# Encoder block in split fp32: who orders the instructions of the vector, scalar and GpSimd engines, which kind of PSUM bank each product takes, and when a block's first half is summed

## The chip, the cores and the metric

The kernel runs on one core of a Trainium2 chip. The metric is the device time of one execution in microseconds (us); lower is better. In the profile PE is TensorE, DVE is VectorE, ACT is ScalarE, POOL is GpSimd, and SP is SyncE, whose queue issues nearly all DMA transfers.

## The reference

One layer of a hybrid bidirectional encoder block: S = 256 tokens, D = 2048, DFF = 5632, all in float32. Cut to what matters:

```python
h = rms_norm(x, g_mix)
proj = h @ w_in                       # q, k, v of three mixers, and three gates of width D
oa, ob, oc = ...                      # dilated windows (6 heads), GQA with rope (6), cross attention to mem (4)
merged = sigmoid(gate_a) * (oa @ w_br_a) + sigmoid(gate_b) * (ob @ w_br_b) + sigmoid(gate_c) * (oc @ w_br_c)
x = x + merged @ w_o
hf = rms_norm(x, g_ffn) @ w_ffn_in    # 2048 x 11264
x = x + (silu(hf[..., :DFF]) * hf[..., DFF:]) @ w_ffn_out
```

Cross attention reads keys and values from `rms_norm(mem, g_mem) @ w_mem_kv`.

## The kernel before

**Arithmetic.** Every fp32 operand is split into a rounded high part and a rest (`split`): ACT copies to `hi` (in the trace `whi`, `x1T`, `hT` and so on), then DVE subtracts and writes `lo` (`wlo`, ...). A product is three matmuls into one PSUM bank: hi by hi, hi by lo, lo by hi. All weights stream through: `load` brings 512 KB (128 x 1024) into one of six buffers `raw` on SP's queue, `halves` splits it into `whi` and `wlo` (four buffers each). So each load costs ACT one copy, DVE one subtraction and PE twelve matmuls of 128x512, or fewer.

**Stages.** `beginning` (keys and values from `mem`); eight products for q, k, v, with the attention running beside them, and four products for the gates and the first branch; then `merging`, `projecting` (x plus merged by `w_o`, and x transposed into `x1T`) and `feeding`. `feeding` handles 11 blocks of `w_ffn` in groups of 4, 4 and 3; behind each group two pairs of column blocks of `w_ffn_out` are added to x.

**A pair.** `pair()` computes two column blocks of 512 at once for two token tiles, so four results: Y and V of the first column block (c = 0), Z and Q of the second (c = 1). It yields steps. A step `d` loads 128x1024 of weights for one column block and issues twelve matmuls: one d-step for Y, V, then one for Z, Q. In the blocks of `w_ffn` three of the contraction's eight parts (`SEVEN = 3`) go by seven products in place of eight: s-steps come in threes, *first* (banks X and Y), *second* (W and Z, from DVE's sums of loaded weights: `t3`, then `raw`, then `t2`), *third* (V, from one more DVE sum); steps 6 and 7 feed X from `t2` and `t3`. The order of a block is `d3 s0 d4 s1 d5 s2 6 d6 7 d7`. `SA` and `SB` hold X's and W's parts; at the end of a pair `finish_seven` adds Y, V, Z and Q to them, all four after the last step. Then `done` is called (in feeding: `hidden`, which applies silu to the first half and starts a side job: multiply the halves, then `transposed`, two groups of four 128x128 PE transposes through a bank `tp`, each emptied by ACT and DVE into `hT`).

**What sets the order.** `run()` prepares three steps ahead (`AHEAD`): a step's loads, splits and sums are issued three steps before its matmuls. `tick()` after each step moves one side job on; a job's `yield n` lets n steps pass. While `run()` runs, `nc` is the wrapper `InOrder` with `on` true: each instruction of all five engines is kept behind the one issued before it on the same engine (`keep_in_program_order`; every instruction of the trace so carries line L70 of the wrapper). The twelve products between `beginning` and `merging` are not in `run()`: there the Tile scheduler orders the engines, by a simulated timeline. Within an engine's queue instructions issue in order, so one that waits holds all behind it.

**Banks.** PSUM has eight banks, in two kinds of four that rotate: `at` and `mm`. A pair takes X, Y and W from `at` and Z, V and Q from `mm`; `tp` takes `at`. A bank is free for its next user once it is emptied.

**The beginning.** Side jobs beside the pair for `mem`: `constants` (after 10 steps: a load of `rope`, a memset of `relb` by DVE, then the load of `relb`, which waits for the memset), and `fetch(xT, 1)`, which loads and splits x transposed, for the qkv products, from step 8 on.

## Time and profile before

| | |
|---|---|
| median of 3 runs | 1478.7 us (1476.6 to 1480.47) |
| the profiled execution | 1478.82 us, span 1477.0 us, mean granted TensorE clock 0.992 |
| busy in the span | PE 1422.2 us, DVE 969.8, ACT 732.4, POOL 76.6 |
| loads of `w_ffn` | 176 of 512 KB, 3.9 us to landing (median) |
| one block of `w_ffn` | 46.4 us (the first d7 matmul at 851.43, the next block's at 897.85) |

Times in rows of the profile count from the span's start. A PE row's duration is modelled; how far matmuls are apart is read from the starts. `[1.36 <-DVE hT L70]` behind a row says that the engine was idle for 1.36 us before it, and that the last thing it waited for was DVE's instruction writing `hT`. Buffer numbers are left out of names in the profile (`hT_7051` is `hT`, `t3_6997` is `t`), and kept in the order's rows below.

### The profile page before, as it was taken

How to read it: one execution, taken by the hardware profiler on the slowest of the kernel's cores; microseconds unless marked ns; L12 is line 12 of the kernel's file. 1: busy time of each engine (PE TensorE's matmuls, PEld its weight loads, DVE VectorE, ACT ScalarE, POOL GpSimd, SP SyncE). 2: the span in 40 equal slices, each digit the busy share in tenths (PEclk: the TensorE clock that was granted, in tenths of full speed). 3: DMA queues.
4: the chain of work that ended last, by engine and by line, in shares of the span. 5: the costliest groups of instructions: out<-in, count | busy, mean ns of one | idle time of the engine just before them, and what ended most of it. 6: DMA issues, size and time to landing. Idle time of an engine off the chain costs nothing.

```text
span 1477.0 us, 17243 instructions
## 1 busy us (share of the span) xinstructions
PE 1422.2 (96%) x6323; PEld 1152.0 (78%) x6323; DVE 969.8 (66%) x1190; ACT 732.4 (50%) x981; POOL 76.6 (5%) x146
## 2 busy tenths in 40 slices
PE   8899999999999999999799999999999999999998
PEld 6678888888788888888577777887777788777776
DVE  5567777754454555646768887557888754788753
ACT  6656565544344444444455545335545533455532
POOL 0012733100000000000000000000000000000000
PEclk9999999999999999999899999999999999999999
DMA  7875455556566666655356556656555566555634
GB/s 273 318 239 186 156 164 165 157 173 197 184 188 197 196 189 190 238 174 196 100 163 208 171 173 204 194 170 201 174 187 178 188 201 196 179 173 179 210 102 169
DMA packets 79411, 277.05 MB, mean 188 GB/s; under 512 B 8992, under 2 KB 11552, under 8 KB 79072
## 3 DMA queue, kind: packets, MB, share of 16 engines
q1 hardware_dynamic: 79184, 275.94, 58.0%
q8 instruction: 49, 0.80, 0.2%
q14 instruction: 34, 0.28, 0.1%
q10 hardware_dynamic: 144, 0.02, 0.0%
HBM read 273.05 MB, written 2.88 MB: 187 GB/s over the span
## 4 chain that ended last, share of the span: by engine, by line
PE 79%; DVE 10%; ACT 6%; DMA 3%; issue 2%; POOL 1%; SPq 0%; ACTq 0%; DVEq 0%
PE mm L70 17%; PE mmY L70 15%; PE mmZ L70 14%; PE mmV L70 14%; PE mmQ L70 13%; DVE wlo L70 5%; ACT whi L70 5%; PE mmX L70 3%; DVE SA L70 1%; PE tp L70 1%; DMA raw<-in_w_mem 1%; PE mmW L70 1%; PE sc L70 1%; DMA rows<-in_x 1%; PE o L70 1%
## 5 line engine op out<-in xcount | busy, mean ns | idle before, releaser
L70 DVE TENSOR_TENSOR wlo<-raw,whi 128x1024 fp32r<-128x1024 f32 (+1 forms) x529 | 630.8, 1203 | 431.2 <-ACT whi L70 428.6
L70 ACT ACTIVATE whi<-raw 128x1024 fp32r<-128x1024 f32 (+1 forms) x529 | 537.7, 1032 | 581.1 <-PE mmQ L70 155.6
L70 PE MATMUL mm<-whi,xT 128*128 128x512 f32 x768 | 245.6, 395 | 3.4 <-ACT xT L70 3.4
L70 PEld LDWEIGHTS mm<-whi,xT 128*128 128x128 f32 x768 | 144.0, 189 | 34.2 <-ACT xT L70 3.8
L70 PE MATMUL mm<-wlo,xT 128*128 128x512 f32 x384 | 151.0, 394 | 0.8 <-DVE wlo L70 0.8
L70 PE MATMUL mmV<-whi,x1T 128*128 128x512 f32 x286 | 112.8, 395 | 0.0
L70 PE MATMUL mmY<-whi,x1T 128*128 128x512 f32 x286 | 112.8, 394 | 0.0
L70 PE MATMUL mmZ<-whi,x1T 128*128 128x512 f32 x220 | 85.7, 389 | 0.0
L70 PE MATMUL mmQ<-whi,x1T 128*128 128x512 f32 x220 | 85.6, 389 | 0.0
L70 PEld LDWEIGHTS mm<-wlo,xT 128*128 128x128 f32 x384 | 72.5, 189 | 16.0 <-DVE wlo L70 1.1
L70 PE MATMUL mmQ<-whi,hT 128*128 128x512 f32 x176 | 69.7, 396 | 2.0 <-DVE x L70 2.0
L70 PE MATMUL mmZ<-whi,hT 128*128 128x512 f32 x176 | 70.2, 399 | 1.1 <-ACT whi L70 1.1
L70 PE MATMUL mmY<-whi,hT 128*128 128x512 f32 x176 | 69.4, 394 | 0.0
L70 PE MATMUL mmV<-whi,hT 128*128 128x512 f32 x176 | 69.1, 393 | 0.0
L70 PEld LDWEIGHTS mmV<-whi,x1T 128*128 128x128 f32 x286 | 54.3, 190 | 11.3 <-ACT whi L70 0.4
L70 PE MATMUL mmY<-wlo,x1T 128*128 128x512 f32 x143 | 58.2, 407 | 4.5 <-DVE wlo L70 3.3
L70 PEld LDWEIGHTS mmY<-whi,x1T 128*128 128x128 f32 x286 | 54.0, 189 | 10.5
L70 PE MATMUL mmV<-wlo,x1T 128*128 128x512 f32 x143 | 56.7, 396 | 0.2 <-DVE wlo L70 0.2
L70 PE MATMUL mmY<-whi,xT 128*128 128x512 f32 x128 | 50.0, 391 | 0.0
L70 PE MATMUL mmZ<-whi,xT 128*128 128x512 f32 x128 | 50.0, 390 | 0.0
L70 PE MATMUL mmV<-whi,xT 128*128 128x512 f32 x128 | 49.8, 389 | 0.0
L70 PE MATMUL mmQ<-whi,xT 128*128 128x512 f32 x128 | 49.8, 389 | 0.0
(243 smaller groups left out, 2463.3 us busy)
## 6 DMA issues: line engine op xcount, KB each, us to landing
raw<-in_w_ffn SPq DMA_DIRECT2D x176, 512.0 KB, 3.9
raw<-in_w_gate SPq DMA_DIRECT2D x96, 512.0 KB, 4.0
raw<-in_w_ffn_out SPq DMA_DIRECT2D x88, 512.0 KB, 3.7
raw<-in_w_qkv SPq DMA_DIRECT2D x64, 512.0 KB, 4.4
raw<-in_w_o SPq DMA_DIRECT2D x32, 512.0 KB, 3.6
raw<-in_w_br SPq DMA_DIRECT2D x24, 512.0 KB, 3.7
raw<-in_w_mem SPq DMA_DIRECT2D x16, 512.0 KB, 6.3
rawT<-in_memT SPq DMA_DIRECT2D x8, 256.0 KB, 4.0
```

The costliest lines, as they stand in the source:

```text
L70: ins = op(*args, **kw)
```

## The change

1. `InOrder` wraps only TensorE and SyncE. DVE, ACT and POOL instructions are the scheduler's to order everywhere; PE's and SP's stay as written in `run()`.
2. X, Y and Z take `at` banks; V, Q and W take `mm` banks.
3. The second transpose group (`h = 1`) takes an `mm` bank while `nc.on`, the first an `at` bank.
4. `finish_seven` becomes `sums(c)`: Y and V are added to `SA` after the last step but one, Z and Q to `SB` after the last, each followed by `done(c, ...)`, both under `tc.high_priority()`. So silu is issued for the first half a step sooner, and the multiplication waits one step instead of two (`yield 1`), which puts both transpose groups a step forward.
5. `fetch(xT, 1)` starts after 5 steps instead of 8.

```diff
-        for name in ("tensor", "vector", "scalar", "gpsimd", "sync"):
+        for name in ("tensor", "sync"):
             setattr(self, name, self._Engine(self, getattr(tc.nc, name)))
+        for name in ("vector", "scalar", "gpsimd"):
+            setattr(self, name, getattr(tc.nc, name))
...
-            tp = bank("tp")
+            tp = bank("tp", "mm" if h and nc.on else "at")
...
-                ps[b] = bank("mm" + b, "at" if b in "XYW" else "mm")
+                ps[b] = bank("mm" + b, "at" if b in "XYZ" else "mm")
...
-        def finish_seven():
-            SA, SB = tl["A"], tl["B"]
-            nc.vector.tensor_sub(SB[:, 0], ps["Z"], SB[:, 0])
-            nc.vector.tensor_add(SA[:, 1], ps["V"], SA[:, 1])
-            nc.vector.tensor_add(SA[:, 0], ps["Y"], SA[:, 0])
-            nc.vector.tensor_add(SB[:, 1], ps["Q"], SB[:, 1])
-            return SA, SB
+        def sums(c):
+            if not seven:
+                return [ps[b] for b in ("YV", "ZQ")[c]]
+            to = tl["AB"[c]]
+            (nc.vector.tensor_sub if c else nc.vector.tensor_add)(to[:, 0], ps["YZ"[c]], to[:, 0])
+            nc.vector.tensor_add(to[:, 1], ps["VQ"[c]], to[:, 1])
+            return to
...
+            def ending(products=products, c=i + 2 - len(steps)):
+                products()
+                with tc.high_priority():
+                    done(c, sums(c))
+            yield ending
...
-        start(hold(8, fetch(xT, 1)))
+        start(hold(5, fetch(xT, 1)))
...
-                def hidden(av, bv):
+                def hidden(c, v, av=halves_of):
+                    if c == 0:
+                        av.append(v)
+                        for t in range(T):
+                            nc.scalar.activation(v[:, t], v[:, t], AF.Silu, scale=r_f[:, 0, t:t + 1])
+                        return
...
-                        yield 2
+                        yield 1
                         nc.vector.tensor_mul(av, av, bv)
```

Before, `pair` called `done(*finish_seven())` after the last step of a pair with seven products, and `done(0, ...)` and `done(1, ...)` after the last two steps of the others, as now.

**DVE at the boundary between two blocks of `w_ffn`.** Before, from the first sum for the next block's first s-step on (`SA<-SA,SB` is the product of the halves; `hT` rows empty the transposes; `[waits DMA...]` is a wait for a load):

```order
L70 TENSOR_TENSOR t3_6997<-raw_7029 128x512 [waits DMAHW1_49]
L70 TENSOR_TENSOR raw_7029<-raw_7029,raw_7027 128x512 [waits DVE_49]
L70 TENSOR_TENSOR t2_6996<-raw_7029 128x512 [waits DVE_49]
L70 TENSOR_TENSOR wlo_7058<-raw_7029,whi_7057 128x1024 [waits Activation_49]
L70 TENSOR_TENSOR SA_6906<-SA_6906,SB_6907 128x1024
L70 TENSOR_TENSOR raw_7027<-t2_6996,raw_7027 128x512 [waits DVE_49]
L70 TENSOR_TENSOR wlo_7078<-raw_7027,whi_7077 128x512 [waits Activation_49]
L70 TENSOR_TENSOR wlo_7098<-raw_7095,whi_7097 128x1024 [waits DMAHW2_49,Activation_49]
L70 TENSOR_TENSOR hT_7051<-tp_7108,hT_7051 128x512 [waits Activation_49]
L70 TENSOR_TENSOR wlo_7118<-raw_7115,whi_7117 128x1024 [waits DMAHW3_49,Activation_49]
L70 TENSOR_TENSOR wlo_7133<-raw_7128,whi_7132 128x1024 [waits DMAHW4_49,Activation_49]
L70 TENSOR_TENSOR hT_7051<-tp_7139,hT_7051 128x512 [waits Activation_49]
```

And now, from the second half's sums on:

```order
L375 TENSOR_TENSOR SB_6907<-mmZ_6724,SB_6907 128x512 [waits PE_49]
L376 TENSOR_TENSOR SB_6907<-mmQ_6728,SB_6907 128x512 [waits PE_49]
L433 TENSOR_TENSOR raw_7031<-t2_6996,raw_7031 128x512 [waits DVE_49]
L417 TENSOR_TENSOR t3_6997<-raw_7137 128x512 [waits DMAHW5_49]
L109 TENSOR_TENSOR wlo_7059<-raw_7033,whi_7058 128x1024 [waits Activation_49]
L777 TENSOR_TENSOR SA_6906<-SA_6906,SB_6907 128x1024 [waits DVE_49]
L418 TENSOR_TENSOR raw_7137<-raw_7137,raw_7135 128x512 [waits DMAHW4_49,DVE_49]
L109 TENSOR_TENSOR wlo_7078<-raw_7031,whi_7077 128x512 [waits Activation_49]
L109 TENSOR_TENSOR wlo_7105<-raw_7102,whi_7104 128x1024 [waits DMAHW2_49,Activation_49]
L419 TENSOR_TENSOR t2_6996<-raw_7137 128x512 [waits DVE_49]
L109 TENSOR_TENSOR hT_7053<-tp_7095,hT_7053 128x512 [waits Activation_49]
L109 TENSOR_TENSOR wlo_7118<-raw_7115,whi_7117 128x1024 [waits DMAHW3_49,Activation_49]
```

The sums `t3`, `raw`, `t2` of the block's first s-step have moved forward, ahead of the last step's sums; in their place stands the first of the next s-step (`t3_6997<-raw_7137`), which waits for a load, ahead of a slice and the product.

**PE at the same boundary.** Before, from the first transpose group to the second:

```order
L70 MATMUL tp_7108<-ident_77,SA_6906 128x128 x2
L70 MATMUL mmW_7121<-whi_7057,fh_5731 128x512 [waits Activation_49]
L70 MATMUL mmW_7121<-wlo_7058,fh_5731 128x512
L70 MATMUL mmW_7121<-whi_7057,fl_5732 128x512
L70 MATMUL mmZ_7081<-whi_7057,fh_5731 128x512
L70 MATMUL mmZ_7081<-wlo_7058,fh_5731 128x512
L70 MATMUL mmZ_7081<-whi_7057,fl_5732 128x512
L70 MATMUL mmV_7065<-whi_7077,x1T_5185 128x512 [waits Activation_49]
L70 MATMUL mmV_7065<-wlo_7078,x1T_5185 128x512 [waits DVE_49]
L70 MATMUL mmV_7065<-whi_7077,x1T_5185 128x512
L70 MATMUL tp_7139<-ident_77,SA_6906 128x128 [waits DVE_49]
L70 MATMUL tp_7139<-ident_77,SA_6906 128x128 x3
```

And now, first where the first group begins, then where the second stands:

```order
L70 MATMUL mmQ_7085<-whi_7011,x1T_5186 128x512
L70 MATMUL tp_7095<-ident_77,SA_6906 128x128 [waits DVE_49,Activation_49]
L70 MATMUL tp_7095<-ident_77,SA_6906 128x128 [waits Activation_49]
L70 MATMUL tp_7095<-ident_77,SA_6906 128x128 x2
L70 MATMUL mmX_7108<-whi_7035,x1T_5185 128x512
L70 MATMUL mmX_7108<-wlo_7036,x1T_5185 128x512
```

```order
L70 MATMUL mmZ_7081<-whi_7058,fh_5731 128x512
L70 MATMUL mmZ_7081<-wlo_7059,fh_5731 128x512
L70 MATMUL mmZ_7081<-whi_7058,fl_5732 128x512
L70 MATMUL tp_7128<-ident_77,SA_6906 128x128 x4
L70 MATMUL mmV_7066<-whi_7077,x1T_5185 128x512 [waits Activation_49]
L70 MATMUL mmV_7066<-wlo_7078,x1T_5185 128x512 [waits DVE_49]
```

Each group has moved a step forward, the first ahead of X and Y, the second ahead of V, and the second group's wait for DVE's eviction is gone.

**DVE in the beginning.** Before, the memset of `relb` is row 35, behind the slices of the `mem` pair:

```order
L70 TENSOR_TENSOR wlo<-raw,whi 128x1024 [waits DMAHW7_49,Activation_49]
L70 TENSOR_TENSOR wlo<-raw,whi 128x1024 [waits DMAHW2_49,Activation_49]
L70 SCALAR_TENSOR_TENSOR memT<-rawT,gT,memT 128x256 [waits DMAHW0_49,Activation_49]
L70 SCALAR_TENSOR_TENSOR memT<-rawT,gT,memT 128x256 [waits Activation_49]
L70 TENSOR_TENSOR wlo<-raw,whi 128x1024 [waits DMAHW4_49,Activation_49]
L70 MEMSET relb 64x6
```

And now:

```order
L266 MEMSET two 128x1
L277 MEMSET relb 64x6
L112 SCALAR_TENSOR_TENSOR memT<-rawT,gT,memT 128x256 [waits DMAHW1_49,DMAHW0_49,Activation_49]
L112 SCALAR_TENSOR_TENSOR memT<-rawT,gT,memT 128x256 [waits Activation_49]
L109 TENSOR_TENSOR wlo<-raw,whi 128x1024 [waits DMAHW2_49,Activation_49]
```

The memset stands at the queue's head, so the load of `relb` on SP's queue no longer waits for it. In the same way, at the last pair, the sums that empty Z and Q of the pair before (`x<-mmZ`, `x<-mmQ`) stand one row ahead of the slice that they stood behind, and in the gate stage the slices behind 381 us stand ahead of the two products `mg<-mm,sg`. Where `projecting` passes into `feeding`, the DVE rows that empty the first transpose into `x1T` now stand behind sums `t3` and `raw` of the first s-steps, and X of the first s-step takes the bank that they empty.

More of the change, by code (lines that the diff above doesn't have):

```diff
@@ L462, in pair @@
             products = ready()
-            if i + 1 < len(steps) and (seven or i + 2 < len(steps)):
+            if i + 2 < len(steps):
                 yield products
-            elif i + 2 == len(steps):
-                def last_but_one(products=products):
-                    products()
-                    done(0, [ps[b] for b in "YV"])
-                yield last_but_one
-            else:
-                def last(products=products):
-                    products()
-                    done(*finish_seven()) if seven else done(1, [ps[b] for b in "ZQ"])
-                yield last
+                continue
+            def ending(products=products, c=i + 2 - len(steps)):
[3 more added lines that the diff above has]
+            yield ending
     def run(pairs):
@@ L762, in feeding @@
             for n in range(c0, c1):
-                def hidden(av, bv):
+                halves_of = []
+                def hidden(c, v, av=halves_of):
[4 more added lines that the diff above has]
+                        return
+                    av, bv = av[0], v
                     tl = s8([P, 2, 4, S], "hT", pool=tail)
                     hT.append(tl)
-                    for t in range(T):
-                        nc.scalar.activation(av[:, t], av[:, t], AF.Silu, scale=r_f[:, 0, t:t + 1])
                     def later():
-                        yield 2
+                        yield 1
                         nc.vector.tensor_mul(av, av, bv)
```

## The prediction

> **What bounds the kernel now.** First the page's head and the chain of work that ended last, then the busy time of PE by stretches, then PE's waits, then single rows.

> ```profile
> span 1477.0 us, 17243 instructions
> ...
> PE 1422.2 (96%) x6323; PEld 1152.0 (78%) x6323; DVE 969.8 (66%) x1190; ACT 732.4 (50%) x981; POOL 76.6 (5%) x146
> ...
> PE 79%; DVE 10%; ACT 6%; DMA 3%; issue 2%; POOL 1%; SPq 0%; ACTq 0%; DVEq 0%
> ```

> PE is the bound: 96% busy, 79% of the chain. The change adds and removes no instruction, so it can give back only PE's 54.8 us of idling (1477.0 - 1422.2) and the time that PE runs at a lower granted clock. Where these lie (columns: stretch; its length, PE busy (instructions), granted clock, DMA share, GB/s):

> ```profile
> 40.00:80.00 40.00, 33.89 (x135) 0.91 0.83 307
> 360.00:400.00 40.00, 38.24 (x169) 1.00 0.58 186
> 400.00:680.00 280.00, 280.00 (x1258) 1.00 0.62 196
> 680.00:720.00 40.00, 35.53 (x157) 0.95 0.44 145
> 720.00:760.00 40.00, 34.01 (x129) 0.87 0.52 160
> 760.00:1400.00 640.00, 619.30 (x2699) 1.00 0.58 185
> 1400.00:1440.00 40.00, 37.96 (x170) 1.00 0.35 116
> 1440.00:1477.00 37.00, 31.11 (x127) 0.95 0.46 170
> ```

> Five places lose time: the passage from the beginning to the qkv products (40 to 80), one wait near 381, the passage from projecting to feeding (680 to 760), the feeding blocks (760 to 1400) and the last pair (1400 on). The stretch 400 to 680, merging and most of projecting, loses nothing although it is pinned too: the change can't gain there. The lower clock is visible in single rows (start, duration):

> ```profile
> 719.59 0.63 PE L70 MATMUL mmV<-wlo,x1T 128*128 128x512 f32 x1
> 720.02 0.63 PE L70 MATMUL mmV<-whi,x1T 128*128 128x512 f32 x1
> ...
> 850.07 0.39 PE L70 MATMUL mmX<-whi,fh 128*128 128x512 f32 x1
> 850.30 0.39 PE L70 MATMUL mmX<-wlo,fh 128*128 128x512 f32 x1
> ```

> At full clock matmuls start 0.23 us apart, after the long waits 0.43. What a lower clock costs in a stretch is its length times (1 - clock): 3.6 us in 40 to 80, 2.0 and 5.2 in 680 to 760, 1.9 in the last. A drawn matmul lasts 0.39 for a pace of 0.23, so each wait costs about 0.16 more than the idling drawn. PE's waits in the feeding blocks, 760 to 1400 (us in total, times, longest):

> ```profile
> PE tp L70 <- DVE hT L70: 10.8, 8, 1.4
> PE mmY L70 <- DVE wlo L70: 3.3, 8, 0.5
> PE mmX L70 <- DVE wlo L70: 2.8, 10, 0.3
> PE tp L70 <- DVE SA L70: 2.6, 8, 0.3
> ```

> **Feeding blocks, the largest term.** At each of 8 boundaries between blocks the second transpose waits for VectorE to empty the first one's bank. One boundary (PE, then VectorE; in brackets the idling before, and its releaser), and how long a weight load of such a block takes to land:

> ```profile
> 862.31 0.39 PE L70 MATMUL mmX<-whi,x1T 128*128 128x512 f32 x1
> 864.16 0.63 PE L70 MATMUL tp<-ident,SA 128*128 128x128 f32 x4 [0.33 <-DVE SA L70]
> 868.23 0.66 PE L70 MATMUL tp<-ident,SA 128*128 128x128 f32 x4 [1.36 <-DVE hT L70]
> ...
> 853.79 1.22 DVE L70 TENSOR_TENSOR wlo<-raw,whi 128x1024 fp32r<-128x1024 f32 x1
> 862.79 1.22 DVE L70 TENSOR_TENSOR SA<-SA,SB 128x1024 f32<-128x1024 f32 x1
> 867.49 0.69 DVE L70 TENSOR_TENSOR hT<-tp,hT 128x512 fp32r<-128x512 f32 x1
> ...
> DMA to landing us min/median/max: 3.4/4.0/5.4
> ```

> What is lost here has two bounds. From the waits: 10.8 + 3.3 + 2.8 + 2.6 = 19.5, and 34 times 0.16, is 25. From the counts: 400 to 680 ran 1258 matmul records in 280 us, 4.49 a us, so 2699 would take 601 of 640: 39 lost (an upper end: records can be missing, and pauses after a wait count). I take 32, their middle.

> Afterwards the second transpose has a bank of the other kind: its 10.8 and 8 times 0.16, 12 us, go. What X and Y wait for now (6.1 and 18 times 0.16, 9 us) are slices that stand behind the boundary's sums and evictions on VectorE; unpinned, the adds into t3, raw and t2 move forward into its idle places, and the slices are in time. I leave 2 of the 9, since the t3 add of a block's last s-step still waits for its load. The first transpose moves a step forward, right behind the first half-block, where X starts at 862.31 now, and its product SA must then be ready. The new VectorE order sets a t3 add ahead of the product that waits for a load. That load can be issued when the slice of 853.79 is done (855.0) and lands 3.4 to 5.4 later (858.4 to 860.4); behind the add (0.6) stand a slice (1.14 to the next) and the product (1.22): ready at 861.4 to 863.4, against 862.3. The wait is between nothing and 1.1; I take its middle, 0.55, with its 0.16 some 6 us for 8 boundaries, where 4 stand now. Of the 7 that 32 has over the waits, 2 stay. After: 2 + 6 + 2 = 10. Gain 22; ends 12 (25 less 2, 9 for waits of 1.1, and 2) and 30. Silu a step earlier lies on ACT, 50% busy, and costs nothing; nor does POOL's freedom, 5% busy.

> **Beginning.**

> ```profile
> 46.83 0.06 DVE L70 MEMSET relb<- 64x6 f32 x1
> ...
> 46.94 0.34 SPq L70 DMA_DIRECT2D relb<-in_rel_bias  x1
> 47.33 0.42 SPq L70 DMA_DIRECT2D raw<-in_w_mem  x1
> ...
> 52.32 0.50 PE L70 MATMUL mmZ<-whi,memT 128*128 128x512 f32 x1 [1.14 <-ACT whi L70]
> ...
> 66.80 0.50 PE L70 MATMUL mm<-whi,xT 128*128 128x512 f32 x1 [3.43 <-ACT xT L70]
> ```

> SP's queue stood until 46.94 because the relb load waited for a memset pinned behind VectorE's slices; the weight load behind it came at 47.33 and Z waited at 52.32. Unpinned, the memset is VectorE's second instruction. The loads of xT start earlier (hold 5 for 8), which takes the wait of 66.80. Lost now: 40 - 33.89 = 6.1, and 3.6 of clock, 9.7. I leave 1: the queue moves 307 GB/s here, and earlier xT loads push others back by at most one 512 KB load (0.42 of issue). Gain 9; ends 5 (the clock's part and one wait stay) and 10.

> **Near 381.** One Y waits 1.76 for a slice that stood behind two gate products on VectorE; the slices now stand ahead. PE idles 40 - 38.24 = 1.8 there: gain 2.

> ```profile
> 381.38 0.50 PE L70 MATMUL mmY<-wlo,xT 128*128 128x512 f32 x1 [1.76 <-DVE wlo L70]
> ```

> **Projecting to feeding.** 680 to 760 loses 4.5 + 6.0 idling and 7.2 of clock, 17.7, of which some 1 belongs to the first block.

> ```profile
> 715.17 0.47 PE L70 MATMUL mmW<-whi,fh 128*128 128x512 f32 x1 [2.84 <-DVE x1T L70]
> 718.28 1.08 PE L70 MATMUL tp<-ident,x 128*128 128x128 f32 x4 [1.24 <-DVE x1T L70]
> 732.13 0.80 PE L70 MATMUL mmW<-whi,fh 128*128 128x512 f32 x1 [3.84 <-ACT whi L70]
> ```

> W leaves the transposes' banks and its wait goes; 732.13 goes, as its adds move forward. But X of the first s-step now takes the first transpose's bank, whose eviction stands on VectorE behind t3 and raw adds that wait for loads, and the last transpose waits for another eviction. The nearest rows are 2.84 and 3.84: two waits of 4 (3.84 + 0.16) and one slow stretch, half of the 7.2: 11.6 after, gain 5; ends 0 and 10.

> **Last pair.**

> ```profile
> 1437.18 1.22 DVE L70 TENSOR_TENSOR wlo<-raw,whi 128x1024 fp32r<-128x1024 f32 x1 [5.36 <-ACT whi L70]
> 1438.33 0.74 DVE L70 SCALAR_TENSOR_TENSOR x<-mmZ,scales,x 128x512 f32<-128x512 f32 x1
> 1439.13 0.50 PE L70 MATMUL mmQ<-whi,hT 128*128 128x512 f32 x1 [2.04 <-DVE x L70]
> ```

> Q waits for a bank; the sum that frees it was ready but pinned behind a slice whose load was late. Now the sums stand ahead. Gone: 2.0 here, the 1.9 of clock, and some 1 of the last stretch's 5.9 of idling (37 - 31.11): SP's next loads stand behind the stores of these sums, which now leave earlier. Gain 5; ends 2 (the wait alone) and 7.

> **The sum.** 22 + 9 + 2 + 5 + 5 = 43; I take off 2 for waits that a queue ordered on assumed landing times makes elsewhere (qkv and gates). 1478.8 - 41 = 1437.8, and the median of the runs, 1478.7, gives the same: 1437.

> On the clock the rows say: the last stretch fell to 0.95 after a wait of 2.04, while 1.76 at 381 left it at 1.00. [...]

> **The rivals.**

> *A VectorE queue that blocks.* The unpinned order sets adds that wait for loads ahead of slices that are ready, in 33 s-steps. In order, one late load stops everything behind it. For: the adds now come up to 5.4 (landing) ahead of need. Against: VectorE's busy 66% and slack of several us in most steps. It decides where each of the 33 adds costs PE 1.4 us (46 over 41 and the threshold): 1484, 5%.

> *The first transpose takes over.* If its product is late by 863.4 or more and the X and Y waits only move, blocks gain 9 instead of 22: 1451. For: VectorE's margin at that place is the smallest of the run, nothing to 1.1 us. 14%.

> *All places clear*, the transition too, and blocks at their upper end: 41 + 8 + 5 = 54, some 1425: 8%.

> *The blocks don't change*: 19 gained elsewhere, 1460: 5%. *The scheduler ends where the hand order did*: 1478: 3%.

> **How the numbers follow.** The likeliest case, 1426 to 1448, has 65%: 1437. About 0.3% (4.4 us) can be told from no change: within it, the last rival and a slice of the first, 3%; slower 4%; faster 93%. The range 1422 to 1457 leaves out the first rival, the last two, and the far side of the best case: 17%.

> **What would show it.** No wait of a tp for hT in the changed profile; tp for SA at 0.5 to 1 each; no mm wait for xT near 66; the relb load before 30; X waiting for x1T once near 705 to 715; clock 1.00 after 1440. Wrong if PE waits for wlo at 20 places or more of over 1 us, if the granted clock in 760 to 1400 falls, or if the transition loses over 18.

## The result, and the profile after

The changed kernel took 1432.2 us (median of 4 runs, 1431.05 to 1433.08) against 1479.3 for the kernel before in the same session: a ratio of 0.9684 with a 95% interval of 0.9667 to 0.9700, 47 us less. The forecast was 1437, range 1422 to 1457. The profiled execution took 1433.08, with a span of 1431.3.

The head of its page:

```profile
span 1431.3 us, 17192 instructions
...
PE 1402.3 (98%) x6323; PEld 1152.6 (81%) x6323; DVE 959.5 (67%) x1190; ACT 741.3 (52%) x981; POOL 76.7 (5%) x146
```

Each engine has as many instructions as before; the total is 51 lower (17243 before), and the page doesn't say of what. PE's idling fell from 54.8 to 29.0 us (1431.3 - 1402.3). PE by stretches (stretch; length, busy, granted clock, DMA share, GB/s), to be set beside the rows of the prediction:

```profile
40.00:80.00 40.00, 39.44 (x176) 1.00 1.02 367
120.00:360.00 240.00, 235.59 (x1148) 0.99 0.52 162
360.00:400.00 40.00, 40.00 (x178) 1.00 0.65 199
680.00:760.00 80.00, 74.34 (x330) 0.98 0.54 167
760.00:1360.00 600.00, 594.21 (x2642) 1.00 0.61 195
1400.00:1431.00 31.00, 25.44 (x109) 1.00 0.37 138
```

Three of these stretches in the kernel before, taken in the same way:

```profile
120.00:360.00 240.00, 239.10 (x1190) 1.00 0.54 171
680.00:760.00 80.00, 69.54 (x285) 0.91 0.48 152
760.00:1360.00 600.00, 581.75 (x2536) 1.00 0.58 184
```

Idling, and length times (1 - clock), give the gain by place. Beginning: 6.1 + 3.6 before, 0.6 now, gain 9.1. The wait near 381: 1.8, gone. Projecting to feeding: 10.5 + 7.2 before, 5.7 + 1.6 now, gain 10.4. Feeding: 106 PE records (the number in brackets) more in the same 600 us, at 4.49 a us a gain of 23.6. The last pair: 2.0 + 5.9 + 1.9 before, 5.6 now, gain 4.2. New is a loss in the qkv and attention stage, 120 to 360: 3.5 of idling and 2.4 of clock. The sum is 43. The spans differ by 45.7; 1360 to 1400, left out above, idled 2.5 before (PE 37.55 of 40) and doesn't now.

PE's waits now (total, times, longest), first those of the feeding blocks, then two others of the whole run:

```profile
PE tp L70 <- DVE SA L777: 5.8, 7, 1.7
...
PE hT L70 <- POOL rot L550: 2.9, 3, 1.7
PE mmX L70 <- DVE rs_h L118: 1.0, 1, 1.0
```

The waits for `hT`, and X's and Y's for `wlo`, are gone from the blocks. In their place the first transpose waits for the product `SA`. One boundary of the changed kernel in the timeline, PE and then DVE:

```profile
842.87 0.63 PE L70 MATMUL tp<-ident,SA 128*128 128x128 f32 x4 [0.57 <-DVE SA L777]
846.07 0.60 PE L70 MATMUL tp<-ident,SA 128*128 128x128 f32 x4
...
839.76 0.69 DVE L417 TENSOR_TENSOR t<-raw 128x512 f32<-128x512 f32 x1 [0.37 <-DMA raw<-in_w_ffn]
840.37 1.22 DVE L109 TENSOR_TENSOR wlo<-raw,whi 128x1024 fp32r<-128x1024 f32 x1
841.50 1.22 DVE L777 TENSOR_TENSOR SA<-SA,SB 128x1024 f32<-128x1024 f32 x1
```

This is the chain that the prediction drew: the `t3` add (`t<-raw`) waits for its load, a slice and the product follow, PE waits for the product. The second transpose comes 3.2 us behind the first and waits for nothing. One sign did not come: the load of `relb`, expected before 30, was issued at 39.46, although its memset ran at 0.83.

### The profile page after: what moved, and what is told of

It reads as the page before. It is cut to its first block, busy times and chain, and to the rows that moved or that the text cites. A ratio compares the mean times of both kernels' runs of the same rounds, so it can differ in the third digit from the quotient of the medians.

```text
span 1431.3 us, 17192 instructions
## 1 busy us (share of the span) xinstructions
PE 1402.3 (98%) x6323; PEld 1152.6 (81%) x6323; DVE 959.5 (67%) x1190; ACT 741.3 (52%) x981; POOL 76.7 (5%) x146
## 4 chain that ended last, share of the span: by engine, by line
PE 80%; DMA 7%; DVE 5%; issue 3%; POOL 2%; ACT 2%; SPq 0%; DVEq 0%; ACTq 0%; POOLq 0%
PE mm L70 17%; PE mmY L70 14%; PE mmZ L70 14%; PE mmV L70 14%; PE mmQ L70 13%; DMA raw<-in_w_ffn 4%; PE mmX L70 3%; DVE wlo L109 2%; DMA raw<-in_w_mem 2%; PE mmW L70 2%; ACT whi L108 1%; PE tp L70 1%; PE sc L70 1%; DVE SA L777 1%; POOL rot L550 1%
## 5 line engine op out<-in xcount | busy, mean ns | idle before, releaser
L108 ACT ACTIVATE whi<-raw 128x1024 fp32r<-128x1024 f32 (+1 forms) x529 | 543.7, 1035 | 584.0 <-PE mmQ L70 202.9
L70 PE MATMUL mm<-whi,xT 128*128 128x512 f32 x768 | 244.6, 395 | 0.0
L70 PEld LDWEIGHTS mm<-whi,xT 128*128 128x128 f32 x768 | 144.5, 189 | 29.8 <-issue 0.8
L70 PE MATMUL mm<-wlo,xT 128*128 128x512 f32 x384 | 151.3, 394 | 0.0
L70 PE MATMUL mmV<-whi,x1T 128*128 128x512 f32 x286 | 112.8, 394 | 0.0
L70 PE MATMUL mmY<-whi,x1T 128*128 128x512 f32 x286 | 111.5, 390 | 0.0
L70 PE MATMUL mmZ<-whi,x1T 128*128 128x512 f32 x220 | 85.7, 390 | 0.0
L70 PE MATMUL mmQ<-whi,x1T 128*128 128x512 f32 x220 | 85.6, 389 | 0.0
L70 PEld LDWEIGHTS mm<-wlo,xT 128*128 128x128 f32 x384 | 72.7, 189 | 15.7 <-issue 0.8
L70 PE MATMUL mmZ<-whi,hT 128*128 128x512 f32 x176 | 69.2, 393 | 1.0 <-ACT whi L108 1.0
L70 PE MATMUL mmY<-whi,hT 128*128 128x512 f32 x176 | 69.6, 396 | 0.0
L70 PE MATMUL mmQ<-whi,hT 128*128 128x512 f32 x176 | 69.1, 393 | 0.0
L70 PE MATMUL mmV<-whi,hT 128*128 128x512 f32 x176 | 69.1, 392 | 0.0
L70 PEld LDWEIGHTS mmY<-whi,x1T 128*128 128x128 f32 x286 | 53.7, 188 | 11.4
L70 PEld LDWEIGHTS mmV<-whi,x1T 128*128 128x128 f32 x286 | 54.0, 189 | 11.0
L70 PE MATMUL mmV<-wlo,x1T 128*128 128x512 f32 x143 | 55.9, 391 | 0.0
L70 PE MATMUL mmY<-wlo,x1T 128*128 128x512 f32 x143 | 55.9, 391 | 0.0
L109 DVE TENSOR_TENSOR wlo<-t,whi 128x1024 fp32r<-128x1024 f32 (+1 forms) x44 | 41.0, 954 | 15.9 <-ACT whi L108 15.9
L70 PE MATMUL mmY<-whi,xT 128*128 128x512 f32 x128 | 50.0, 391 | 0.0
L70 PE MATMUL mmZ<-whi,xT 128*128 128x512 f32 x128 | 50.0, 390 | 0.0
L70 PE MATMUL mmV<-whi,xT 128*128 128x512 f32 x128 | 49.8, 389 | 0.0
```

Source lines behind the costliest of these rows:

```text
L70: ins = op(*args, **kw)
L108: nc.scalar.activation(hi, src, AF.Copy)
L109: nc.vector.tensor_sub(lo, src, hi.bitcast(F32))
```

## The experiments

Theory A was the prediction's: the free order of VectorE takes away the waits of the beginning, 381, the last pair, and X and Y; the second transpose's 12 us go because it has a bank of another kind. Rivals: the free order alone does it; parts 2 to 5 alone do it.

**Part 1 alone** (`unpin_only`), on the kernel before:

```diff
-        for name in ("tensor", "vector", "scalar", "gpsimd", "sync"):
+        for name in ("tensor", "sync"):
             setattr(self, name, self._Engine(self, getattr(tc.nc, name)))
+        for name in ("vector", "scalar", "gpsimd"):
+            setattr(self, name, getattr(tc.nc, name))
```

> The kernel before with part 1 alone: VectorE, ScalarE and GpSimd are the scheduler's, banks, sums and transposes as before. Theory A (the order on VectorE was behind the waits of the beginning, of 381, of the last pair and of X and Y, 24 us; the bank of the second transpose is a matter by itself): the second transpose still waits for hT at the 8 boundaries (about 11 us), the rest goes: 1450 to 1458. Rival B (with a free VectorE order the eviction also comes earlier, and the banks matter little): 1436 to 1442. Rival C (free order without the new banks collides: X and W wait for the transposes' banks): over 1465.

1434.6 us (1431.6 to 1435.1), ratio 0.9696 (0.9681 to 0.9710). One part gives 45 of the 47 us; theory A, with 1450 to 1458, gave it 15 to 23 less. The two intervals overlap, so what parts 2 to 5 add to it together can't be told from nothing. Rival B came near with its 1436 to 1442, but its reason doesn't hold, since the wait for the eviction is still there:

```profile
PE tp L70 <- DVE hT L109: 11.4, 8, 1.9
```

What theory A had missed shows in two stretches:

```profile
680.00:760.00 80.00, 74.24 (x329) 0.98 0.55 172
760.00:1360.00 600.00, 589.32 (x2613) 1.00 0.61 192
```

The passage to feeding gains 10 (5.8 idling and 1.6 clock left), which theory A had left out, and the blocks gain 77 records, 17 us, with the wait for `hT` still in them: the free order takes X's and Y's waits whole and more.

**Parts 2 to 5 alone** (`pin_all`), on the changed kernel:

```diff
-        for name in ("tensor", "sync"):
+        for name in ("tensor", "vector", "scalar", "gpsimd", "sync"):
             setattr(self, name, self._Engine(self, getattr(tc.nc, name)))
-        for name in ("vector", "scalar", "gpsimd"):
-            setattr(self, name, getattr(tc.nc, name))
```

> The changed kernel with all five engines pinned again: parts 2 to 5 alone. Theory A: the beginning, 381, the last pair and the X and Y waits come back (24 us), the second transpose's 12 us stay gone: 1454 to 1462. Rival B (parts 2 to 5 carry the gain, the unpinning only rides along): 1432 to 1442. Rival C (early transposes need the free order, pinned they wait): over 1470.

1500.5 us, ratio 1.0145 (1.0130 to 1.0160): 21 us slower than the kernel before. Rival C has the figure; the waits are others than it named. Its longest waits of PE in the feeding blocks and two stretches, then DVE's rows at one boundary:

```profile
PE mmY L70 <- DVE wlo L70: 10.2, 16, 0.8
PE mmW L70 <- DVE wlo L70: 5.3, 7, 0.8
```

```profile
120.00:360.00 240.00, 234.39 (x1157) 0.99 0.52 163
760.00:1360.00 600.00, 581.35 (x2498) 1.00 0.58 182
```

```profile
871.43 1.23 DVE L70 TENSOR_TENSOR SA<-SA,SB 128x1024 f32<-128x1024 f32 x1
...
875.25 1.23 DVE L70 TENSOR_TENSOR wlo<-raw,whi 128x1024 fp32r<-128x1024 f32 x1 [0.54 <-ACT whi L70]
```

No transpose of the blocks waits here, as parts 3 and 4 had it. But pinned, the product now stands ahead of the three adds that make W's weights; the slice for W comes 3.8 us after the product's start, and W and Y wait in the transposes' stead, 15.5 us. 38 records fewer than before in 760 to 1360 are 8.5 us of the 21, and 120 to 360 idles 5.6 instead of 0.9 with 2.4 of clock, 7 more. So parts 2 to 5 cost time under a written order; which of them costs how much no pinned run took apart.

**The second transpose on an `at` bank again** (`tp_at`), on the changed kernel:

```diff
-            tp = bank("tp", "mm" if h and nc.on else "at")
+            tp = bank("tp")
```

> The changed kernel with the second transpose on an 'at' bank as before (part 3 undone). Theory A: the wait for hT returns at 8 boundaries with about 1.4 us each, part of it under the wait for SA: 1440 to 1446. Rival: VectorE, free, empties the first transpose in time, and nothing returns: 1430 to 1435.

1431.8 us, ratio 0.9685 (0.9669 to 0.9701): no difference. Theory A's price for this bank, 12 us, is wrong in this kernel.

**Both transposes a step later** (`yield2`), on the changed kernel:

```diff
                     def later():
-                        yield 1
+                        yield 2
                         nc.vector.tensor_mul(av, av, bv)
```

> The changed kernel with both transposes a step later (yield 2 in place of 1), the rest as changed. Theory A (the first transpose now waits for the product SA because it was moved a step forward): the 6.8 us of waits for SA go, 1425 to 1428. Rival: the later evictions stand behind slices on VectorE and the waits move to the d-steps or to hT: 1431 to 1437.

1423.6 us, ratio 0.9625 (0.9611 to 0.9640): 8.6 us faster than the changed kernel. The waits of its feeding blocks:

```profile
PE mmY L70 <- DVE wlo L109: 1.7, 3, 0.7
PE mmZ L70 <- DVE wlo L109: 0.8, 1, 0.8
PE tp L70 <- DVE SA L777: 0.4, 1, 0.4
```

The wait for `SA` came from the step forward, as theory A had it; waits of Y and Z, 2.5 us, take part of its place. Not all of the 8.6 us is the step's. The blocks run 18 records more from 760 to 1360 (2660 against 2642), 4.0 us. From 120 to 360 the clock is 1.00 here and 0.99 in the changed kernel, 2.4 us, in a stage before the edit begins; `tp_at`, the same there as the changed kernel, has 1.00 too, so that part is the clock's and not the step's.

Why, then, did the bank not count? With `yield 1` the steps X, Y and W, Z stand between the groups, 12 matmuls; with `yield 2`, as before, W, Z and V, 9 matmuls. Theory D: the bank matters only where the eviction doesn't fit between.

**Yield 2 and the `at` bank** (`y2_tp_at`): the two edits above together.

> The version with both transposes a step later (yield 2), and the second one on an 'at' bank again. With yield 1 the bank made no difference; there 12 matmuls stand between the two groups, here 9. Theory D (the bank matters only where the eviction of the first group doesn't fit between the groups): the wait for hT returns at 8 boundaries, 8 to 12 us: 1431 to 1436. Rival (VectorE's free order empties the bank in time by itself): 1422 to 1426.

1438.0 us, ratio 0.9724 (0.9700 to 0.9748): 14.4 us over `yield2`. Its PE instructions stand in the same order as `yield2`'s. The wait for `hT` is back, 10.9 us in 8 times over the whole run, as theory D had it; the time is above its 1431 to 1436. Part of the 14.4 lies elsewhere: from 760 to 1360 this one runs 40 records fewer than `yield2` (2620 against 2660), 8.9 us for 7 of the 8 boundaries, and 120 to 360 has the clock at 0.99 again. The pairs of transposes, first of `tp_at`, then of `yield2`, then of this one, and in `tp_at` and here DVE's eviction of the first:

```profile
839.91 0.63 PE L70 MATMUL tp<-ident,SA 128*128 128x128 f32 x4 [0.81 <-DVE SA L777]
843.36 0.66 PE L70 MATMUL tp<-ident,SA 128*128 128x128 f32 x4
...
842.63 0.68 DVE L109 TENSOR_TENSOR hT<-tp,hT 128x512 fp32r<-128x512 f32 x1
```

```profile
838.24 0.60 PE L70 MATMUL tp<-ident,SA 128*128 128x128 f32 x4
840.75 0.60 PE L70 MATMUL tp<-ident,SA 128*128 128x128 f32 x4
```

```profile
843.44 0.60 PE L70 MATMUL tp<-ident,SA 128*128 128x128 f32 x4
847.60 0.66 PE L70 MATMUL tp<-ident,SA 128*128 128x128 f32 x4 [1.47 <-DVE hT L109]
...
846.86 0.68 DVE L109 TENSOR_TENSOR hT<-tp,hT 128x512 fp32r<-128x512 f32 x1
```

With a bank of its own the second group follows 2.5 us behind the first over 9 matmuls, and 3.2 over 12 (the changed kernel). On a shared kind it starts only once the first is emptied (DVE's row ends 0.05 us ahead of it in `tp_at`, 0.06 here): over 12 matmuls it comes 3.45 behind, next to no wait, and over 9 it comes 4.16 behind. The spacing is only half of that. The eviction itself ends 3.40 us behind the first group's start in `tp_at` and 4.10 here, where one slice more stands between the product and it on DVE. Were it so late in `tp_at`, 12 matmuls would not cover it either.

**xT from step 8 again** (`y2_hold8`), on `yield2`:

```diff
-        start(hold(5, fetch(xT, 1)))
+        start(hold(8, fetch(xT, 1)))
```

> The version with yield 2, and xT fetched from step 8 on as before (part 5 undone). Theory E (the earlier xT moves the qkv products forward and the attention's chain comes too late for PE, some 5 us between 140 and 196): 40 to 80 loses up to 2 more, the attention gives back 4 to 5: 1420 to 1424. Rival F (the earlier start of xT is what took the wait at 66.80 and its slow clock away): 5 to 9 us more: 1428 to 1433. Rival G (neither, order freedom alone did it): 1422 to 1425 with the attention's loss unchanged.

1418.3 us (1417.3 to 1420.3), ratio 0.9592 (0.9573 to 0.9611), the fastest of all: 5.3 us under `yield2` (4.9 by the ratios, whose intervals just meet). Theory E holds, save that 40 to 80 lost nothing; from 80 to 150 PE runs 6 records fewer (328 against 334), 1.3 us. PE in `yield2`, then here:

```profile
40.00:80.00 40.00, 39.73 (x177) 1.00 1.02 373
120.00:360.00 240.00, 235.55 (x1159) 1.00 0.54 165
```

```profile
40.00:80.00 40.00, 39.73 (x176) 1.00 0.97 351
120.00:360.00 240.00, 238.76 (x1183) 1.00 0.54 166
```

The beginning's gain is the free order's; the earlier fetch isn't needed for it, and it costs 3.2 us of the attention's time (the waits for `rot` fall from 3.0 to 0.5). The prediction had counted it among the gains.

**VectorE pinned again** (`pin_dve`), and **ScalarE pinned again** (`pin_act`), each on the changed kernel with the other two engines free:

```diff
-        for name in ("tensor", "sync"):
+        for name in ("tensor", "sync", "vector"):   # pin_act: "scalar"
```

> The changed kernel with VectorE pinned again, ScalarE and GpSimd free. Theory (VectorE's written order is what made PE wait): close to the version with all pinned, 1490 to 1502. Rival (ScalarE's order carries it, since each slice waits for its copy): 1435 to 1450.

> The changed kernel with ScalarE pinned again, VectorE and GpSimd free. Theory (VectorE's order carries the gain): 1432 to 1440. Rival (a copy pinned behind another makes its slice late whatever VectorE's order): 1465 to 1500.

1480.9 us (1.0019, 1.0008 to 1.0031) and 1446.8 us (0.9786, 0.9766 to 0.9807). In the changed kernel VectorE's freedom is worth 48.7 us, ScalarE's 14.6. Each theory had the right sign and neither its figure: with VectorE pinned, free ScalarE and GpSimd still save 20 us against all pinned, and ScalarE pinned comes out above the 1440 expected. ScalarE's order costs in two places. ACT's row at a boundary of `pin_act`, PE's wait in its blocks, and PE in its beginning:

```profile
843.30 1.34 ACT L70 ACTIVATE SA<-SA,scales 128x512 f32<-128x512 f32 x2 [2.73 <-DVE SA L375]
```

```profile
PE mmY L70 <- DVE wlo L109: 8.8, 15, 0.8
...
40.00:80.00 40.00, 37.19 (x145) 0.91 0.91 338
```

Silu, issued a step sooner, waits 2.73 us for the sum with the next copy queued behind it, and that copy's slice is late for Y. The prediction priced silu's step at nothing because ACT is 50% busy; that is so only where ScalarE's order is free. The blocks lose 33 records from 760 to 1360 (2609 against 2642), 7.3 us. The beginning loses about as much: 2.8 of idling and 3.6 of clock against 0.6 in the changed kernel, where Z waits for copies (`whi`) and slices.

Three of the last four runs ask which parts `y2_hold8` needs, and one tries a further edit.

**Parts 1 and 3 alone** (`unpin_tp`): `unpin_only`, and `bank("tp", "mm" if h and nc.on else "at")`.

> The kernel before with parts 1 and 3 alone: free order of VectorE, ScalarE and GpSimd, and the second transpose on an 'mm' bank; X, Y and W on 'at', sums after the last step, xT from step 8. Theory (free order plus a bank of its own is all that the gain needs): the 11.4 us of waits for hT that the version with part 1 alone kept are gone, 1420 to 1425. Rival (Z, V, Q and the transpose now fill all four 'mm' banks, and the next block's Z or V waits for an eviction): 1429 to 1436.

1427.6 us, ratio 0.9660 (0.9645 to 0.9675), between theory and rival. The waits for `hT` are gone, 7 us are gained on `unpin_only`. The blocks gain more, 57 records from 760 to 1360 (2670 against 2613), 12.7 us; 640 to 760 gives some back (492 against 512, 4.5 us). What is left over `y2_hold8` is the next run's.

**X, Y, W on `at`** (`b_w_at`), on `y2_hold8`:

```diff
-                ps[b] = bank("mm" + b, "at" if b in "XYZ" else "mm")
+                ps[b] = bank("mm" + b, "at" if b in "XYW" else "mm")
```

> The version with yield 2 and xT from step 8, and X, Y, W on 'at' with Z, V, Q on 'mm' again (part 2 undone). Theory (with free order each bank is emptied in time; only the passage from projecting to feeding feels it, where W takes a transpose's bank): 1417 to 1422. Rival (four users of 'mm' at each boundary, Z, V, Q and the transpose, collide): 1426 to 1434.

1428.1 us, ratio 0.9657 (0.9641 to 0.9673), 10 us over `y2_hold8` and the same as `unpin_tp`. The figure is the rival's, but the boundaries don't collide (2673 records from 760 to 1360, 2667 in `y2_hold8`). The place is projecting and its passage to feeding, near where the theory looked, though no W waits there. One stretch of PE and the wait that is new, here, then the stretch in `y2_hold8`:

```profile
640.00:760.00 120.00, 112.40 (x493) 0.96 0.50 160
...
663.55 1.09 PE L70 MATMUL tp<-ident,x 128*128 128x128 f32 x4 [2.94 <-DVE x1T L112]
```

```profile
640.00:760.00 120.00, 114.99 (x521) 1.00 0.56 176
```

From 640 to 760 this one loses 7.6 of idling and 4.8 of clock, the other 5.0: 7.4 us, where the two spans differ by 6.9. The wait at 663.55 is a transpose's, of a second group in projecting, and `unpin_tp` has it too (2.94 at 663.38); `unpin_only`, whose transposes all take `at`, does not. There Z, V, Q and the second group share the four `mm` banks: the rival's collision, it seems, but in projecting. That it is the bank's kind and not DVE's order was not tried apart.

**Sums after the last step** (`b_late`), on `y2_hold8`; pairs with seven products call `done` for both halves at the end:

```diff
                 products()
+                if seven and c == 0:
+                    return
                 with tc.high_priority():
-                    done(c, sums(c))
+                    if seven:
+                        both = [sums(0), sums(1)]
+                        done(0, both[0])
+                        done(1, both[1])
+                    else:
+                        done(c, sums(c))
```

> The version with yield 2 and xT from step 8, and both halves' sums and silu issued after a block's last step (the earlier sums of part 4 undone). Theory (VectorE and ScalarE, free, place the sums by readiness, and when they are issued matters little): 1416 to 1421. Rival (the first half's banks are free a step later, and the product SA later): 1422 to 1430.

1420.7 us, ratio 0.9610 (0.9595 to 0.9624). The intervals overlap: the earlier sums are worth 2.4 us by the medians and perhaps nothing, as the theory had it.

**Four steps between the last transposes of projecting** (`b_lag4`), on `y2_hold8`: the lag of `transposed` in `projecting` is `4 if n else 2` instead of 2.

> The version with yield 2 and xT from step 8, and the last two column blocks of projecting transposed with four steps between their groups instead of two. Theory (the wait of 2.6 us before the last transpose, and the slow clock behind it, come from a bank whose eviction isn't through): both go, 1412 to 1415. Rival (VectorE is what is late there, the wait moves to the next X or W): 1416 to 1420.

1421.4 us, ratio 0.9614 (0.9600 to 0.9628): a miss, no gain, and above the rival's figure too. The wait grew and stayed with the same transpose:

```profile
709.91 1.09 PE L70 MATMUL tp<-ident,x 128*128 128x128 f32 x4 [3.60 <-DVE rs_t L125]
...
708.09 1.21 DVE L109 TENSOR_TENSOR wlo<-raw,whi 128x1024 fp32r<-128x1024 f32 x1
...
709.29 0.47 DVE L112 SCALAR_TENSOR_TENSOR x1T<-tp,gT,x1T 128x256 fp32r<-128x256 f32 x1
```

More matmuls as cover did not help: DVE's evictions into `x1T` stand between slices and adds there, the last one ends at 709.76, just ahead of the transpose. So VectorE seems to be what is late, as the rival said, though the wait stayed where it was. (The small `rs_t` row that the view names only ran last.) Whether an order with these evictions first would take the wait away wasn't tried.

## Why the prediction was right or wrong

**The sum** was right: 41 us forecast, 47 measured by the medians, and the time within the range. Its terms:

- *Beginning*, 9: measured 9.1. The reasons were too narrow. The fetch's part fell with `y2_hold8`. The memset's place isn't enough: in `pin_act` the memset runs at 0.83 as in the changed kernel, and the stretch still loses 6.4. With VectorE pinned (`pin_dve`) the memset runs at 55.47 and the stretch loses 12.8 (PE 32.41 of 40, clock 0.87). So the beginning's gain needs VectorE and ScalarE both free.
- *Near 381*, 2: measured 1.8; *last pair*, 5: measured 4.2.
- *Feeding blocks*, 22: measured 23.6 over 600 us. The size held, the working did not. "Its 10.8 and 8 times 0.16, 12 us, go" because of the bank of the other kind was the step that failed: in this kernel the bank is worth nothing (`tp_at`). The wait went because the earlier step puts 12 matmuls between the groups instead of 9, and because DVE's eviction ends sooner there (3.40 us behind the first group's start; 4.02 in the kernel before). With 9 between, the bank is worth 12.7 in the blocks (`unpin_tp` over `unpin_only`) and 14.4 in all (`y2_tp_at` over `yield2`), about the price that was put on it: the size fit, and that the same 12 us went by another cause was luck. X and Y, where 2 us were left, wait for nothing now, and that is the free order's (`unpin_only`). The first transpose's wait was put at 0.55 a boundary, bounds nothing to 1.1; it came out at 0.83 (5.8 in 7, one of them 1.7), through the rows that were named.
- *Projecting to feeding*, 5: measured 10.4. Mis-sized: the two waits were taken at 4 us each and came out at 1.0 and 2.6, with 1.6 us of clock instead of 3.6.
- *Waits elsewhere*, 2: measured some 6, all in the attention stage. The cause found for 3.2 of them is the earlier fetch, priced at one load; 2.4 are a slow clock that `tp_at` and `yield2` don't have there.

**The rivals.** VectorE's queue does block on loads as the first rival said, but by 0.77 us a time. No PE matmul of the blocks waits for a slice, so away from the boundaries this stays within its slack; at the boundaries it is part of the first transpose's wait:

```profile
DVE t L417 <- DMA raw<-in_w_ffn: 18.4, 24, 1.8
```

The first transpose did become the wait of the blocks, the second rival's mechanism, without taking the X and Y waits along. That the change could be slower was true of its parts: pinned, parts 2 to 5 cost 21 us. The prediction counted parts 3 and 5 as gains and the step forward as 2 us of cost (6 where 4 stood), and had no rival in which the parts beside the free order are worth nothing that can be measured, which is what `unpin_only` shows.

**The clock.** The prediction read from two rows that the clock fell behind a wait of 2.04 us and not behind one of 1.76. As a threshold for one wait that doesn't hold: in the changed kernel a wait of 2.64 has the clock at 0.50 behind it, in `y2_hold8` one of 2.65 has 1.00. First the changed kernel, then `y2_hold8` at the same place, each with PE in two stretches of 3.41 us (length, busy, clock):

```profile
712.11 1.08 PE L70 MATMUL tp<-ident,x 128*128 128x128 f32 x4 [2.64 <-DVE rs_y L126]
...
708.32:711.73 3.41, 1.15 (x5) 1.00 0.13 18
711.73:715.14 3.41, 3.03 (x10) 0.50 0.82 280
```

```profile
706.24 0.63 PE L70 MATMUL tp<-ident,x 128*128 128x128 f32 x4 [2.65 <-DVE rs_y L126]
...
701.72:705.13 3.41, 1.87 (x11) 1.00 0.07 29
705.13:708.54 3.41, 2.30 (x12) 1.00 0.79 232
```

## What to carry to other kernels

Where several engines feed one that must not wait, a written order on all of them can be what makes it wait. Here VectorE's written order alone cost 49 us of 1481 in the changed kernel; no run freed VectorE alone in the kernel before. TensorE and the transfer queue stayed under the wrapper in every run, so whether they need it isn't shown. Before pricing a change of banks, set the work between the two users against the end of the first one's eviction: a bank of its own was worth some 13 us where 9 matmuls were between and the eviction ended 4 us behind, and nothing where 12 were between and it ended 3.4 behind. Take a bundle of edits apart: the transposes' step forward and the earlier fetch cost 14 us together, and the kernel without them, 1418.3 us, beats both.
